# RWKV right sides taken head by head, two chunks in one transposition, and other constants in the order planner

## The chip, the cores and the metric

The kernel runs on one core of one Trainium2 chip. The metric is device time in microseconds (us) of one execution; lower is better. TensorE is called PE here, VectorE DVE, ScalarE ACT, GpSimd POOL and SyncE SP, as in the profile.

## The reference

One inference step of a two-layer encoder, for 528 prompt rows (16 learned meta rows and 512 tokens) and 8 sample streams of 16 rows, all in float32. Each layer computes

```
h = rmsnorm(x); z = h @ w_in                      # one combined projection, 7 input groups
A: RWKV-7 time mixing, 8 heads of 64:
   sa = S @ (-kk);  S = S*decay + sa (kk*a)^T + v k^T;  y = S @ r     # per row
B: latent attention (low-rank K and V, rotary key, QK norm), 8 heads
x += (sigmoid(g_a) * (A @ w_branch_a) + sigmoid(g_b) * (B @ w_branch_b)) @ w_out
```

The prompt starts A from a zero state; each sample stream starts it from its own state (`state_rwkv`, 64x64 for each head), and the final states are outputs. Outputs are also the new caches and the last projected rows.

## The kernel before

All 656 rows (128 sample rows, then the prompt) lie along the free axis, so the activations are tiles of 128 features x 656, cut into halves of 328. The large projections run as three passes in a rounded float format, from a high and a low part of both sides: these are the matmuls on tile `zt` (`main_mm`, line 751), 48 for each 128 output columns of the input projection. Their weights come in as `raw`, ACT and POOL split them into `whi` and `wlo` (`main_split`), and `main_post` (line 789) takes the results out of PSUM. Here this stream is called the main one; everything else is called a side operation.

Branch A runs by pairs of heads, `j` = 0 to 3, beside the main stream. A pair's rows are cut into 11 chunks: chunks 0 and 1 hold 4 sample streams of 16 rows each, chunk 2 the meta rows, chunks 3 to 10 the prompt, 64 rows each. For a pair, `rwkv_prep` makes the scaled keys and decays (tile `ar`) and the chunk matrices `Q`; `rwkv_tok` (line 1476) transposes keys (`kbt`) and values (`vt`, line 1496) into rows by features; `rwkv_inv` inverts the triangular blocks with DVE steps on `LP` and 16- and 32-row matmuls on tile `mg`; `rwkv_chain` (line 1604) walks the prompt chunks (`la`, `so`, `mw`, `ch`); and `rwkv_sample` (line 1724) does chunks 0 and 1:

- The streams' states come in as `sin`, are transposed by four matmuls (PSUM tile `s0`, line 1735; its rows read `s`) and copied by ACT to `S0` (rows read `S`), chunk by chunk.
- The right sides `ra` (line 1741) are a local part, two 64x64 matmuls from `Q` and `SAV` (`local`, line 1592), and a state part, eight matmuls for 4 streams x 2 heads. The state part contracts over 128 rows, both heads' rows at once: the left operand `am` holds zeros in the other head's rows.
- `solve` (line 1582) copies `ra` to `RB` by DVE, multiplies (`sa`), and DVE copies the result into `SAV`. Then come the outputs `yo`, the new states (`sn`, `snew`, `snt`) and their DMAs.

A plain float32 matmul is two passes on PE, so eight matmuls show as 16 instructions; a transposition is one.

What sets the order: while the program is built, class `Clock` plans every engine's order, and that order is then fixed on PE, DVE, ACT and POOL. Each generator is a thread with a rank. At each step the operation that can start first, by the planner's own estimates, is issued; at equal starts a side operation goes ahead of the main stream (rank `MAIN` = 90), then one that needs no other array shape, then the lower rank. One rule turns this round: `lean` (line 388) keeps a sum of the columns PE has done of late. Where a side operation would bring the sum below a floor plus `SPARE`, the planner becomes `tight` and side operations go behind the main stream until the sum is above `AGAIN`. Ranks: pairs `j` (samples `j` + 2.5), the shift rows 4, branch A's norms `RN` = 5, the prompt's attention `RPR` = 5 (`mla_prompt`), the sample's attention 0. The main tasks of a layer come in a fixed order: 23 tasks of the input projection can run during branch A; the gate tasks after them wait for ("rw", l), which is set when all pairs are done (`pre`, line 1045).

PSUM tiles of side operations come from two rings, `s` with 3 banks and `c` with 2 (`PSB`, line 73). `S2` (line 610) takes two banks of ring `s` at once.

Of the kernel before, what the change touches and what calls it, by code (L numbers as in the profile page):

```python
# [10 lines left out]
F32 = mybir.dt.float32  # L11
F32R = mybir.dt.float32r
I32 = mybir.dt.int32
AF = mybir.ActivationFunctionType
ALU = mybir.AluOpType
# [35 lines left out]
DLAT = 1.9  # L51
DRATE = 260e3
MAIN = 90
RPR = 5
RN = 5
RPOST, RSPLIT, RRAW = -3, 0, 2
MARGIN = 0.1
PIN = "PVAG"
TICK = 3.41333
ENTRY = 3100.0  # L60
SPARE = 150.0
AGAIN = 4400.0
GEARLY = 0
GMID = 1
SBB = 1
# [8 lines left out]
CT = "c"  # L74
# [136 lines left out]
class Clock:  # L211
# [176 lines left out]
    def lean(self, o):  # L388
# [8 lines left out]
        if self.tight:  # L397
            self.tight = self.dense(t - TICK) < AGAIN
        elif c < ENTRY + SPARE:
            self.tight = True  # L400
# [171 lines left out]
def trunk_kernel(ctx: ExitStack, tc: tile.TileContext, I, O, dbg=None, nlayers=NL):  # L572
    nc = tc.nc
    clk = Clock(tc)
    V, A, G, TE, SP = (Engine(e, clk, n) for e, n in ((nc.vector, "V"), (nc.scalar, "A"), (nc.gpsimd, "G"), (nc.tensor, "P"), (nc.sync, "S")))
# [17 lines left out]
    def C(name):  # L593
        i, o, n = COFF[name]
        return ctile[i][:, o:o + n]

    ident = C("ident")
# [17 lines left out]

    def S(name="s", tag="s"):
        return pools["PS"].tile([128, 512], F32, tag=tag, name=name, bufs=PSB[tag])
# [17 lines left out]
    def mm(out, lhsT, rhs, start, stop):  # L635
        TE.matmul(out, lhsT, rhs, start=start, stop=stop)
# [729 lines left out]
    def Us(name):  # L1366
        return pools["R"].tile([128, 512], F32, tag="U", name=name, bufs=UR)


    def ccol(c):  # L1370
        return (0, 64, 128)[c] if c < 3 else PR + 64 * (c - 3)
# [104 lines left out]
    def rwkv_tok(l, j):  # L1476
        while ("kb", l, j) not in done:
            yield has(("kb", l, j))
        R = pools["R"]
        kbf, r = st["kbf", j], None  # L1480

        BKT = R.tile([128, 11, 128], F32, tag="BKT", name="BKT", bufs=2)
        st["BKT", j] = BKT
        for cs in ((0, 1, 2, 3), (4, 5, 6, 7), (8, 9, 10)):
            ps = S("kbt")
            for i, c in enumerate(cs):
                TE.transpose(ps[:, 128 * i:128 * i + 128], kbf[:, c, :], ident)
            A.activation(out=BKT[:, cs[0]:cs[-1] + 1, :], in_=ps[:, 0:128 * len(cs)].rearrange("p (a b) -> p a b", b=128), func=AF.Copy)
            yield None
        done.add(("kbt", l, j))  # L1490
        while ("v", l, j) not in done or ("pq", l, j) not in done:
            yield has(("v", l, j), ("pq", l, j))
        v = get(("v", l, j), "K")
        r, SAV = st["r", l, j], st["SAV", j]
        for cs in ((0, 1, 2, 3), (4, 5, 6, 7), (8, 9, 10)):
            ps = S("vt")
            for i, c in enumerate(cs):
                TE.transpose(ps[0:64, 128 * i:128 * i + 128], v[:, ccol(c):ccol(c) + 64], ident)
            A.activation(out=SAV[0:64, cs[0]:cs[-1] + 1].rearrange("p a b c -> p a (b c)"),
                         in_=ps[0:64, 0:128 * len(cs)].rearrange("p (a b) -> p a b", b=128), func=AF.Copy)  # L1500
            yield None

        for hh, (c0, c1) in enumerate(H2):
            ps = S("bo")
            z = [Us("bo")[:, 0:328] for _ in range(2)]
            split(*z, r[:, c0:c1])
            for i in range(2):
                mm(ps[:, 0:328], r_(C("bones")), r_(z[i]), i == 0, i == 1)
            V.tensor_tensor(out=v[:, c0:c1], in0=v[:, c0:c1], in1=ps[:, 0:328], op=ALU.mult)
            yield None  # L1510
        SP.dma_start(out=bod[j], in_=v)
        done.add(("tok", l, j))
# [65 lines left out]
        yield None  # L1578

    PR2 = (slice(0, 64), slice(64, 128))  # L1580

    def solve(j, c, ps):

        Q, SAV = st["Q", j], st["SAV", j]
        rb = pools["R"].tile([128, 128], F32, tag="RB", name="RB", bufs=1)
        V.tensor_copy(out=rb[64:128], in_=ps[64:128, 0:128])
        ps2 = S("sa", CT if c > 1 else "s")
        for p in range(2):
            mm(ps2[64:128, 64 * p:64 * p + 64], Q[64:128, c, p, 0:64], rb[64:128, 64 * p:64 * p + 64], p == 0, p == 1)
        V.tensor_copy(out=SAV[64:128, c].rearrange("p h v -> p (h v)"), in_=ps2[64:128, 0:128])  # L1590

    def local(j, c, ps, stop):
        Q, SAV = st["Q", j], st["SAV", j]
        for p in range(2):
            mm(ps[64:128, 64 * p:64 * p + 64], Q[0:64, c, p, 0:64], SAV[0:64, c, p, :], p == 0, stop and p == 1)

    def chain_y(j, c, ps, n, first):
        Q, SAV = st["Q", j], st["SAV", j]
# [125 lines left out]
    def rwkv_sample(l, j):  # L1724
        R = pools["R"]
        Q, SAV, BKT = st["Q", j], st["SAV", j], st["BKT", j]
        pc = st["pc", j]
        ar = st["ar", j]
        yt = st["y", j]
        for c in range(2):  # L1730
            t = Us("sin")
            for p in range(2):
                SP.dma_start(out=t[0:64].rearrange("v (s h k) -> v s h k", s=4, h=2)[:, :, p],
                             in_=I["state_rwkv"][l, 4 * c:4 * c + 4, 2 * j + p].rearrange("s v k -> v s k"))
            ps = S("s0")
            for s in range(4):
                TE.transpose(ps[:, 64 * s:64 * s + 64], t[0:64, 128 * s:128 * s + 128], ident[0:64, 0:64])
            S0 = R.tile([128, 4, 64], F32, tag="S0", name="S0", bufs=2)
            A.activation(out=S0.rearrange("p s v -> p (s v)"), in_=ps[:, 0:256], func=AF.Copy)
            yield None  # L1740
            ps = S("ra")
            local(j, c, ps, False)
            am = st["am", l]
            for p in range(2):
                V.tensor_copy(out=am[PR2[p], 256 * p:256 * p + 320].rearrange("p (s t) -> p s t", t=80)[:, :, 0:16], in_=ar[PR2[p], 0, 64 * c:64 * c + 64].rearrange("p (s t) -> p s t", t=16))
            for s in range(4):
                for p in range(2):
                    mm(ps[64:128, 64 * p:64 * p + 64], am[:, 256 * p + 64 * s:256 * p + 64 * s + 64], S0[:, s, :], False, p == 1 and s == 3)
            yield None
            solve(j, c, ps)  # L1750
            yield None
            py = S("yo")
            for s in range(4):
                for p in range(2):
                    mm(py[PR2[p], 16 * s:16 * s + 16], S0[PR2[p], s, :], ar[PR2[p], 1, 64 * c + 16 * s:64 * c + 16 * s + 16], s == 0, False)
            chain_y(j, c, py, 64, False)
            A.activation(out=yt[:, 64 * c:64 * c + 64], in_=py[:, 0:64], func=AF.Copy)
            yield None
            sx = Us("sx")
            V.tensor_tensor(out=sx.rearrange("p (h s v) -> p h s v", h=2, v=64),  # L1760
                            in0=SAV[:, c].rearrange("p h (u v) -> p h u v", u=1).to_broadcast([128, 2, 4, 64]),
                            in1=C("rmask").rearrange("p (h s v) -> p h s v", h=1, v=1).to_broadcast([128, 2, 4, 64]), op=ALU.mult)
            psn = S("sn")
            for p in range(2):
                mm(psn[PR2[p], 0:256], BKT[:, c, 64 * p:64 * p + 64], sx[:, 256 * p:256 * p + 256], True, True)
            sn = Us("snew")[:, 0:256]
            o3 = sn.rearrange("p (s v) -> p s v", v=64)
            V.tensor_tensor(out=o3, in0=psn[:, 0:256].rearrange("p (s v) -> p s v", v=64), in1=S0, op=ALU.add)
            G.tensor_tensor(out=o3, in0=o3, in1=pc[:, 4 * c:4 * c + 4].rearrange("p (s u) -> p s u", u=1).to_broadcast([128, 4, 64]), op=ALU.mult)
            yield None  # L1770
            pst = S("snt")
            for s in range(4):
                TE.transpose(pst[0:64, 128 * s:128 * s + 128], sn[:, 64 * s:64 * s + 64], ident)
            so = Us("so")
            A.activation(out=so[0:64], in_=pst[0:64], func=AF.Copy)
            for p in range(2):
                SP.dma_start(out=O[6][l, 4 * c:4 * c + 4, 2 * j + p].rearrange("s v k -> v s k"),
                             in_=so[0:64].rearrange("v (s h k) -> v s h k", s=4, h=2)[:, :, p])
            yield None
        done.add(("samp", l, j))  # L1780
# [694 lines left out]
    def branches(l):  # L2475
# [13 lines left out]
        smp_open(l)  # L2489
        yield from par(mla_sample(l), mla_prompt(l), open_y(l), rank=[0, RPR, 0])  # L2490

# [77 lines left out]
```

## Time and profile before

| | |
|---|---|
| time, median of 3 runs | 1768.52 us (1762.73 to 1777.48) |
| time of the profiled execution | 1768.54 us |
| its span, first to last instruction | 1766.8 us |
| instructions | 38155 |
| mean granted PE clock | 0.954 of full |

In the rows below, the granted clock of 1.00 is 2.4 GHz, and 0.50 is 1.2 GHz. Busy times of PE are modelled ends of pipelined passes, so the start of one group against the start of the next tells what a group costs; the duration shown does not. `128*64` after a matmul is the shape of the array tile that it uses (rows * columns); `(x16)` or `x16` counts instructions. A trailing bracket names idle time before an instruction and what ended it. Branch A of the first layer fills about 88 to 418 us, that of the second about 968 to 1275 us.

### The profile page before, as it was taken

The page shows a single profiled execution, that of the slowest core. Times are in us where ns is not written, and L with a number is a line of the kernel's source. Part 1 is how long each engine was busy: PE and PEld are TensorE (multiplying, and loading weights), DVE is VectorE, ACT ScalarE, POOL GpSimd, SP SyncE. Part 2 cuts the span into 40 slices and gives each one's busy share as a digit, 9 for nine tenths or more (in the row PEclk, how much of TensorE's full clock was granted, in tenths as well). Part 3 has the DMA queues.
Part 4 walks back from the last instruction along what each step waited for, and adds up shares of the span by engine and source line. Part 5 has one row for each costly group of instructions (what it writes and reads, how often), then busy time and mean ns, then how long its engine had stood idle before and what let it go on. Part 6 is the DMA issues. An engine that isn't in the chain of part 4 may idle for free.

```text
span 1766.8 us, 38155 instructions
## 1 busy us (share of the span) xinstructions
PE 1673.0 (95%) x15157; PEld 1507.2 (85%) x15157; DVE 983.8 (56%) x2366; ACT 727.1 (41%) x1704; POOL 578.1 (33%) x590
## 2 busy tenths in 40 slices
PE   7999998999999997999999999899999999899998
PEld 6988777788898996899999878778888999889998
DVE  5686776755552454455336867886456334455441
ACT  4544343443544543223334434455345444432231
POOL 2422122134522533014434212132354244411262
PEclk9998897999999998999999978999999999999999
DMA  6531222235465226365532312232455642356462
GB/s 194 159 112 49 57 77 70 58 108 186 121 215 165 70 72 182 103 176 173 175 107 83 105 35 66 78 91 60 146 180 159 201 124 68 109 164 178 148 211 84
DMA packets 217916, 217.27 MB, mean 123 GB/s; under 512 B 46217, under 2 KB 166481, under 8 KB 217209
## 3 DMA queue, kind: packets, MB, share of 16 engines
q1 hardware_dynamic: 217737, 214.82, 40.4%
q8 instruction: 120, 1.97, 0.5%
q14 instruction: 59, 0.48, 0.1%
HBM read 145.98 MB, written 68.52 MB: 121 GB/s over the span
## 4 chain that ended last, share of the span: by engine, by line
PE 72%; DVE 16%; ACT 4%; issue 3%; DMA 3%; POOL 1%; SPq 1%; DVEq 0%; POOLq 0%; ACTq 0%
PE zt L566 41%; DVE LP L566 3%; PE pv L566 3%; PE st L566 3%; PE mg L566 3%; PE kp L566 3%; PE yo L566 1%; PE pcx L566 1%; PE so L566 1%; PE psc L566 1%; DVE itmp L566 1%; PE pq L566 1%; DVE xs L566 1%; PE ra L566 1%; DMA q<-qpd 1%
## 5 line engine op out<-in xcount | busy, mean ns | idle before, releaser
L566 POOL TENSOR_TENSOR wlo<-raw,whi 128x512 fp32r<-128x512 f32 (+2 forms) x304 | 346.0, 1146 | 669.8 <-ACT whi L566 603.5
L566 PE MATMUL zt<-hhi,whi 128*128 128x328 f32 (+1 forms) x1376 | 453.1, 329 | 6.8 <-ACT whi L566 4.5
L566 PE MATMUL zt<-hhi,wlo 128*128 128x328 f32 (+1 forms) x1376 | 452.7, 329 | 3.6 <-POOL wlo L566 3.6
L566 PE MATMUL zt<-hlo,whi 128*128 128x328 f32 (+1 forms) x1376 | 453.3, 329 | 0.4 <-issue 0.3
L566 PEld LDWEIGHTS zt<-hhi,whi 128*128 128x128 f32 (+1 forms) x1376 | 268.5, 195 | 14.9 <-ACT whi L566 5.4
L566 PEld LDWEIGHTS zt<-hhi,wlo 128*128 128x128 f32 (+1 forms) x1376 | 268.3, 195 | 13.9 <-POOL wlo L566 5.1
L566 PEld LDWEIGHTS zt<-hlo,whi 128*128 128x128 f32 (+1 forms) x1376 | 268.2, 195 | 8.6 <-issue 3.0
L566 ACT ACTIVATE whi<-raw 128x512 fp32r<-128x512 f32 (+2 forms) x304 | 163.7, 551 | 211.6 <-PE zt L566 182.8
L566 DVE TENSOR_TENSOR sg<-zt,rb 128x328 f32<-128x328 f32 x64 | 31.7, 496 | 94.9 <-PE zt L566 94.8
L566 PE MATMUL zt<-mh,wlo 128*128 128x328 f32 x256 | 81.4, 318 | 0.0
L566 PE MATMUL zt<-ml,whi 128*128 128x328 f32 x256 | 80.8, 316 | 0.0
L566 PE MATMUL zt<-mh,whi 128*128 128x328 f32 x256 | 80.2, 313 | 0.0
L566 ACT ACTIVATE xs<-u,vec 128x328 f32<-128x328 f32 x68 | 38.6, 568 | 92.9 <-DVE u L566 90.4
L566 ACT ACTIVATE pT<-st 128x384 f32<-128x384 f32 (+3 forms) x80 | 35.0, 463 | 85.0 <-DVE st L566 48.3
L566 DVE TENSOR_TENSOR kh<-kp,kh 128x272 fp32r<-128x272 f32 x64 | 28.1, 441 | 71.4 <-ACT kh L566 71.2
L566 PE MATMUL st<-q,k 96*128 96x512 f32 (+9 forms) x288 | 65.1, 333 | 1.0 <-DVE st L566 0.6
L566 PE MATMUL zt<-ya,whi 128*128 128x328 f32 x256 | 65.4, 322 | 0.0
L566 DVE SCALAR_TENSOR_TENSOR xs<-u,vec,xs 128x327 f32<-128x327 f32 x68 | 48.2, 709 | 25.4 <-ACT xs L566 19.9
L566 DVE TENSOR_TENSOR xn<-xn,zt 128x328 f32<-128x328 f32 x32 | 15.8, 495 | 77.7 <-PE zt L566 71.4
L566 POOL TENSOR_TENSOR snew<-snew,pc 128x256 f32<-128x256 f32 x16 | 10.8, 672 | 143.1 <-DVE snew L566 143.1
L566 POOL TENSOR_TENSOR sqs<-sqs 128x272 f32<-128x272 f32 x48 | 37.2, 776 | 60.3 <-ACT sqs L566 58.1
L566 PEld LDWEIGHTS pv<-vtok,pT 128*128 128x128 f32 x480 | 55.6, 192 | 0.2
(410 smaller groups left out, 3783.7 us busy)
## 6 DMA issues: line engine op xcount, KB each, us to landing
raw<-in_w_in_dram SPq DMA_DIRECT2D x84, 512.0 KB
raw<-in_w_out_dram SPq DMA_DIRECT2D x16, 512.0 KB
gad<-sg SPq DMA_DIRECT2D x16, 328.0 KB
gbd<-sg SPq DMA_DIRECT2D x16, 328.0 KB
ga<-gad SPq DMA_DIRECT2D x16, 328.0 KB
ya<-yad SPq DMA_DIRECT2D x16, 328.0 KB
mad<-ga SPq DMA_DIRECT2D x16, 328.0 KB
gg<-gbd SPq DMA_DIRECT2D x16, 328.0 KB
```

What stands on the lines that cost most here:

```text
L566: clk.record(n, lambda: f(*a, **kw), outs, ins, c, cols if n == "P" else 0, lock, lane)
```

## The change

Three edits, and constants of the planner:

- `rwkv_tok` transposes the values of two neighbouring chunks at once, 128 columns instead of 64, in 6 instead of 11 transpositions for a pair; ACT takes each chunk from its half of the partitions, in 4 copies instead of 3.
- `rwkv_sample` loads both chunks' states into one tile, chunk 0 in partitions 0 to 63 and chunk 1 in 64 to 127, and transposes both by four matmuls of full height; one ACT copy of 512 columns takes the place of two of 256, and `S0` is one buffer with both chunks.
- The state part of the right sides contracts over 64 rows, each head over its own. Head 0 goes on in the local part's bank (`ps`), head 1 gets a bank of its own (`ps1`). ACT copies `ps` to `RB` and DVE adds `ps1` to head 1's half, where one DVE copy stood.
- `RPR` 5 to 7, `SPARE` 150 to 600, `AGAIN` 4400 to 4800.

```diff
-RPR = 5
+RPR = 7
-SPARE = 150.0
-AGAIN = 4400.0
+SPARE = 600.0
+AGAIN = 4800.0
...
-        for cs in ((0, 1, 2, 3), (4, 5, 6, 7), (8, 9, 10)):
+        for cs in ((3, 5, 7, 9), (0, 2)):
             ps = S("vt")
+            n = len(cs)
             for i, c in enumerate(cs):
-                TE.transpose(ps[0:64, 128 * i:128 * i + 128], v[:, ccol(c):ccol(c) + 64], ident)
-            A.activation(out=SAV[0:64, cs[0]:cs[-1] + 1].rearrange("p a b c -> p a (b c)"),
-                         in_=ps[0:64, 0:128 * len(cs)].rearrange("p (a b) -> p a b", b=128), func=AF.Copy)
+                TE.transpose(ps[:, 128 * i:128 * i + 128], v[:, ccol(c):ccol(c) + 128], ident)
+            p3 = ps[:, 0:128 * n].rearrange("p (a b) -> p a b", b=128)
+            A.activation(out=SAV[0:64, cs[0]:cs[-1] + 1:2].rearrange("p a b c -> p a (b c)"), in_=p3[0:64], func=AF.Copy)
+            m = n if n > 2 else 1
+            A.activation(out=SAV[0:64, cs[0] + 1:cs[0] + 2 * m:2].rearrange("p a b c -> p a (b c)"), in_=p3[64:128, 0:m], func=AF.Copy)
...
-            ps = S("s0")
-            for s in range(4):
-                TE.transpose(ps[:, 64 * s:64 * s + 64], t[0:64, 128 * s:128 * s + 128], ident[0:64, 0:64])
-            S0 = R.tile([128, 4, 64], F32, tag="S0", name="S0", bufs=2)
-            A.activation(out=S0.rearrange("p s v -> p (s v)"), in_=ps[:, 0:256], func=AF.Copy)
-            yield None
-            ps = S("ra")
-            local(j, c, ps, False)
+        ps = S("s0")
+        for s in range(4):
+            TE.transpose(ps[:, 128 * s:128 * s + 128], t[:, 128 * s:128 * s + 128], ident)
+        S0 = R.tile([128, 4, 2, 64], F32, tag="S0", name="S0", bufs=1)
+        A.activation(out=S0.rearrange("p s c v -> p (s c v)"), in_=ps, func=AF.Copy)
+        yield None
+        for c in range(2):
+            ps, ps1 = S2("ra", "ra")
+            for p in range(2):
+                mm(ps[64:128, 64 * p:64 * p + 64], Q[0:64, c, p, 0:64], SAV[0:64, c, p, :], p == 0, False)
...
             for s in range(4):
                 for p in range(2):
-                    mm(ps[64:128, 64 * p:64 * p + 64], am[:, 256 * p + 64 * s:256 * p + 64 * s + 64], S0[:, s, :], False, p == 1 and s == 3)
-            yield None
-            solve(j, c, ps)
+                    mm((ps, ps1)[p][64:128, 0:64], am[PR2[p], 256 * p + 64 * s:256 * p + 64 * s + 64], S0[PR2[p], s, c, :], p == 1 and s == 0, s == 3)
+            yield None
+            rb = R.tile([128, 128], F32, tag="RB", name="RB", bufs=1)
+            A.activation(out=rb[64:128], in_=ps[64:128, 0:128], func=AF.Copy)
+            V.tensor_tensor(out=rb[64:128, 64:128], in0=ps1[64:128, 0:64], in1=rb[64:128, 64:128], op=ALU.add)
+            ps2 = S("sa")
```

The rest of `solve` stands inline as it was, and `solve` and `local` are gone.

## Rows read from the trace of the kernel before

**Rows 1.** the page: engines' busy time, and PE's granted clock in 40 slices
```profile
PE 1673.0 (95%) x15157; PEld 1507.2 (85%) x15157; DVE 983.8 (56%) x2366; ACT 727.1 (41%) x1704; POOL 578.1 (33%) x590
...
PEclk9998897999999998999999978999999999999999
```

**Rows 2.** windows of three stages: us, busy by engine (x instructions), PEclk, DMA
```profile
132.00:352.00 220.00, 202.33 (x2531) 165.84 (x2531) 153.20 (x352) 92.31 (x217) 48.73 (x49) 0.84 0.22 62
...
1012.00:1144.00 132.00, 123.90 (x1617) 101.06 (x1615) 95.26 (x230) 55.05 (x129) 27.77 (x29) 0.86 0.19 55
1144.00:1280.00 136.00, 129.23 (x1648) 106.95 (x1649) 86.87 (x201) 61.81 (x147) 38.68 (x39) 0.99 0.33 99
```

**Rows 3.** the page: chain that ended last, shares of the span by engine
```profile
PE 72%; DVE 16%; ACT 4%; issue 3%; DMA 3%; POOL 1%; SPq 1%; DVEq 0%; POOLq 0%; ACTq 0%
```

**Rows 4.** pieces of the chain of waits, 88 to 400 us: start, us, what
```profile
165.53 0.56 PE vt L566 x4
...
231.96 1.08 PE ra L566 x16
```

**Rows 5.** the same chain, 980 to 1290 us
```profile
1035.23 0.58 PE kbt L566 x4
```

**Rows 6.** timeline, 1258 to 1268 us: start, us, engine, what
```profile
1258.56 0.31 PE L566 MATMUL zt<-hhi,wlo 128*128 128x328 f32 x1
...
1258.70 0.32 PE L566 MATMUL zt<-hhi,whi 128*128 128x328 f32 x1
...
1258.95 0.46 PE L566 MATMUL s<-cst,sin 64*128 64x64 f32 x4
...
1259.34 0.42 PE L566 MATMUL zt<-hlo,whi 128*128 128x328 f32 x1
...
1259.69 0.44 PE L566 MATMUL ra<-QV 64*64 64x64 f32 x4
...
1260.06 0.41 PE L566 MATMUL zt<-hhi,wlo 128*128 128x328 f32 x1
...
1260.40 1.15 PE L566 MATMUL ra<-S,am 128*64 128x64 f32 x16
...
1261.48 0.41 PE L566 MATMUL zt<-hhi,whi 128*128 128x328 f32 x1
...
1261.59 0.29 DVE L566 COPY RB<-ra 64x128 f32<-64x128 f32 x1 [1.67 <-PE ra L566]
```

**Rows 7.** timeline of PE, 384 to 389 us
```profile
384.43 0.27 PE L566 MATMUL so<-LP,QV 64*64 64x128 f32 x1
384.44 0.22 PE L566 MATMUL la<-QV 64*64 64x64 f32 x1
384.54 0.27 PE L566 MATMUL so<-LP,QV 64*64 64x128 f32 x1
```

**Rows 8.** ACT's groups by shape: xcount | busy us, mean ns | idle before
```profile
L566 ACT ACTIVATE LP<-la 64x128 f32<-64x128 f32 x72 | 19.5, 271 | 4.9 <-PE la L566 3.2
...
L566 ACT ACTIVATE QV<-vt 64x512 f32<-64x512 f32 x16 | 9.1, 585 | 1.1 <-PE vt L566 0.9
...
L566 ACT ACTIVATE S<-s 128x256 f32<-128x256 f32 x16 | 6.1, 380 | 6.5 <-PE s L566 6.3
...
L566 ACT ACTIVATE QV<-vt 64x384 f32<-64x384 f32 x8 | 3.9, 481 | 6.1 <-PE vt L566 6.1
```

**Rows 9.** DVE's groups by shape, the one nearest to an addition of 64 columns
```profile
L566 DVE SCALAR_TENSOR_TENSOR SB<-ch,pc,SB 128x64 f32<-128x64 f32 x64 | 17.8, 278 | 5.3 <-PE ch L566 4.4
```

**Rows 10.** windows of 4 us in the first layer's stage
```profile
136.00:140.00 4.00, 2.28 (x73) 2.02 (x71) 3.73 (x7) 1.88 (x6) 1.52 (x2) 1.00 0.46 121
...
144.00:148.00 4.00, 4.00 (x41) 3.59 (x40) 1.98 (x4) 1.31 (x4) 1.97 (x1) 0.50 0.00 0
284.00:288.00 4.00, 1.40 (x11) 1.16 (x11) 3.83 (x5) 1.32 (x3) 0.62 (x1) 1.00 0.51 131
```

**Rows 11.** windows, instructions on zt alone
```profile
88.00:418.00 330.00, 148.27 (x707) 119.09 (x706) 17.75 (x35) 5.22 (x12) 0.90 0.26 76
```

More of the change, by code (lines that the diff above doesn't have):

```diff
@@ L1580, in trunk_kernel @@
     PR2 = (slice(0, 64), slice(64, 128))
[L1582 to L1595, printed above, removed]
     def chain_y(j, c, ps, n, first):
@@ L1729, in rwkv_sample @@
         yt = st["y", j]
+        t = Us("sin")
         for c in range(2):
-            t = Us("sin")
             for p in range(2):
-                SP.dma_start(out=t[0:64].rearrange("v (s h k) -> v s h k", s=4, h=2)[:, :, p],
+                SP.dma_start(out=t[64 * c:64 * c + 64].rearrange("v (s h k) -> v s h k", s=4, h=2)[:, :, p],
                              in_=I["state_rwkv"][l, 4 * c:4 * c + 4, 2 * j + p].rearrange("s v k -> v s k"))
-            ps = S("s0")
-            for s in range(4):
-                TE.transpose(ps[:, 64 * s:64 * s + 64], t[0:64, 128 * s:128 * s + 128], ident[0:64, 0:64])
-            S0 = R.tile([128, 4, 64], F32, tag="S0", name="S0", bufs=2)
-            A.activation(out=S0.rearrange("p s v -> p (s v)"), in_=ps[:, 0:256], func=AF.Copy)
-            yield None
-            ps = S("ra")
-            local(j, c, ps, False)
+        ps = S("s0")
[8 more added lines that the diff above has]
+                mm(ps[64:128, 64 * p:64 * p + 64], Q[0:64, c, p, 0:64], SAV[0:64, c, p, :], p == 0, False)
             am = st["am", l]
@@ L1747, in rwkv_sample @@
                 for p in range(2):
-                    mm(ps[64:128, 64 * p:64 * p + 64], am[:, 256 * p + 64 * s:256 * p + 64 * s + 64], S0[:, s, :], False, p == 1 and s == 3)
+                    mm((ps, ps1)[p][64:128, 0:64], am[PR2[p], 256 * p + 64 * s:256 * p + 64 * s + 64], S0[PR2[p], s, c, :], p == 1 and s == 0, s == 3)
             yield None
-            solve(j, c, ps)
+            rb = R.tile([128, 128], F32, tag="RB", name="RB", bufs=1)
+            A.activation(out=rb[64:128], in_=ps[64:128, 0:128], func=AF.Copy)
+            V.tensor_tensor(out=rb[64:128, 64:128], in0=ps1[64:128, 0:64], in1=rb[64:128, 64:128], op=ALU.add)
+            ps2 = S("sa")
+            for p in range(2):
+                mm(ps2[64:128, 64 * p:64 * p + 64], Q[64:128, c, p, 0:64], rb[64:128, 64 * p:64 * p + 64], p == 0, p == 1)
+            V.tensor_copy(out=SAV[64:128, c].rearrange("p h v -> p (h v)"), in_=ps2[64:128, 0:128])
             yield None
@@ L1754, in rwkv_sample @@
                 for p in range(2):
-                    mm(py[PR2[p], 16 * s:16 * s + 16], S0[PR2[p], s, :], ar[PR2[p], 1, 64 * c + 16 * s:64 * c + 16 * s + 16], s == 0, False)
+                    mm(py[PR2[p], 16 * s:16 * s + 16], S0[PR2[p], s, c, :], ar[PR2[p], 1, 64 * c + 16 * s:64 * c + 16 * s + 16], s == 0, False)
             chain_y(j, c, py, 64, False)
@@ L1767, in rwkv_sample @@
             o3 = sn.rearrange("p (s v) -> p s v", v=64)
-            V.tensor_tensor(out=o3, in0=psn[:, 0:256].rearrange("p (s v) -> p s v", v=64), in1=S0, op=ALU.add)
+            V.tensor_tensor(out=o3, in0=psn[:, 0:256].rearrange("p (s v) -> p s v", v=64), in1=S0[:, :, c, :], op=ALU.add)
             G.tensor_tensor(out=o3, in0=o3, in1=pc[:, 4 * c:4 * c + 4].rearrange("p (s u) -> p s u", u=1).to_broadcast([128, 4, 64]), op=ALU.mult)
```

## The prediction

> **What bounds the kernel now.** I read the page first. PE is busy 95% of the span and no other engine passes 56% [rows 1], so PE's work and PE's clock are the two things to ask about. The row of the granted clock is at 9 or full but for a few slices. The windows by stage place them: in 132 to 352 us the clock is 0.84 and in 1012 to 1144 us 0.86, while 1144 to 1280 us, branch A too, has 0.99 [rows 2]. The two low stretches are in branch A of the two layers, where the three edits lie. The clock has two levels, so a mean of 0.84 over 220 us is 0.16 x 2 x 220 = 70 us at 1.2 GHz, and 0.86 over 132 us is 37 us: 107 us at half rate, worth 54 us of full rate. In the same stretches PE is busy 202.33 of 220 and 123.90 of 132 us, 92% and 94%. So branch A is bound by PE for the most part, with DVE next, and the chain that ended last says the same: PE 72%, DVE 16% [rows 3]. The groups of sixteen `ra` passes stand on that chain: ten of the kernel's 16 are whole pieces of it, eight of them near the 1.08 us of the one that is shown [rows 4], two at half clock longer.
>
> **Right sides.** Two layers, 4 pairs and 2 chunks make 16 groups of 16 state passes. One takes 1.08 us (1260.40 to 1261.48, [rows 6]), 67 ns a pass. Afterwards each pass needs 64 rows, and the heads alternate between the two halves of the array, so two can run together, where both halves write the same output partitions. The trace shows that case: `so` reads the upper rows, `la` the lower ones, both write partitions 64 to 127 of different banks, and `so` starts each 0.11 us with an `la` pass within [rows 7]. An `so` pass moves 128 columns, twice as many as here. If the pair of passes costs those 0.11 us, a group takes 8 x 0.11 = 0.88 us and saves 0.20; if it costs one pass of today, it takes 8 x 0.067 = 0.54 and also saves 0.54. I take 0.54, as 64 columns are what today's passes move too: 16 x 0.54 = 8.6 us. Changes of array shape come on top. From `zt` at 1260.06 to the `ra` group at 1260.40 it is 0.34 us, where a `zt` pass in a row takes 0.14 to 0.15 (1258.56 to 1258.70), so the change costs 0.19 [rows 6]; the local part has a change of its own. With both parts in 64*64 one is saved where they stand together, which the planner decides: between 0 and 16 x 0.19 = 3, I take 1.2. Right sides: 9.8 us, between 3 and 12.
>
> A rule speaks about this edit. The Trainium skill, "TensorEngine Tiling (Array Packing)", Restrictions and Gotchas, says that different row tiles cannot work on one PSUM bank at a time, so that row tiling needs more banks. The pairs in the trace write different tiles, and no run here shows two row halves on one bank. The change gives head 1 its own bank, so by the rule the pairing stands; had both heads shared a bank, the 8.6 us would go and the forecast would be 6 us later.
>
> **States.** A group of four half-height transpositions stands between two `zt` passes: `s` starts at 1258.95, the `zt` behind it at 1259.34 (0.39 us), and 0.10 us of shape change lies before it [rows 6]: 0.49, twice for a pair. Afterwards there are four of full height without a change of shape; four such `kbt` take 0.58 us [rows 5]. That saves 0.98 - 0.58 = 0.40, 8 times: 3.2 us (0 if the trace's 0.49 is mostly drain that stays).
>
> **Values.** Four `vt` take 0.56 us on the chain [rows 4], 0.14 each, and four full ones 0.145 each [rows 5]. A pair had 11 and has 6: 1.54 - 0.87 = 0.67, 8 times: 5.4 us.
>
> **The sum on PE** is 9.8 + 3.2 + 5.4 = 18.4 us, between 8 and 21. Of a saving in a stretch where PE holds 72% of the chain I count 72%: 13.2 us. What is late next, where it doesn't count, is DVE's steps for the inverse, which run with or without these passes.
>
> **ACT and DVE.** For a pair's values ACT keeps two copies of 512 columns, and in place of one of 384 (481 ns) come one of 256 (380, the states' copy is as wide) and one of 128 (271): +0.17 us. For the states 2 x 380 become one of 585: -0.18 us [rows 8]. Together nothing, at an engine that is 41% busy. The right side was taken out by one DVE copy of 295 ns; now an ACT copy of 64x128 (271 ns, [rows 8]) comes first and then a DVE addition of 64x64. The trace has no such addition; the nearest is `SB` with 64 columns from PSUM, 278 ns [rows 9], so I take 0.28, between 0.2 and 0.3. The way to `sa` gets 0.26 us longer, 16 times 4 us. In front of it stand `zt` passes that can run meanwhile (1261.48 and on, behind the copy at 1261.59, [rows 6]); where a stage ends with the last pair's samples that cover thins out, for two chunks in two layers: 4 x 0.26 = 1 us lost. Queued behind the new ACT copy is ACT's weight split for the main stream, later by 0.27 us each time, with two more split buffers ahead of it: nothing, and 16 x 0.27 = 4 us if the main stream were waiting for each.
>
> **DMA and buffers.** The 32 loads of states stay 32; all four of a pair are issued at its start on SP, two earlier than now, ahead of what SP would issue then: nothing. One `S0` buffer in place of two costs nothing, since a pair's samples wait for those of the pair before anyway.
>
> **`RPR` 5 to 7.** Ranks only break ties. While the prompt's heads run, the other threads have rank 0, 2 or below, or 90; the norms with rank 5 end before, because the keys wait for them. No thread lies between 5 and 7, so this does nothing.
>
> **`SPARE` and `AGAIN`.** These put main passes ahead of branch A's sooner and for longer. Where did the clock fall? At 136 to 140 us PE works 2.28 of 4 us, with `mg` passes of 16 and 32 rows behind, and 144 to 148 us is at 0.50; at 284 to 288 us it works 1.40 of 4 [rows 10]. Each fall begins with a gap in which PE had nothing ready, main passes included, while DVE was busy 3.73 and 3.83 us; no order of PE mends that. The half-rate time after it, with main passes and sparse ones mixed, is what a reserve can shorten. Bounds: all 107 us cured gives 54 us; on the other side, 268 us of the second layer (1012 to 1280) at the first layer's 0.84 instead of today's would have 86 us at half rate, where it has 37 + 3, so 23 us lost. That the same program runs at 0.84 in one layer and 0.86 and 0.99 in the other shows how much hangs on the order. I take 5 us gained, near nothing, since the gaps come first.
>
> **Sum.** 13.2 + 5 - 1 = 17 us off the profiled execution's 1768.54 (a span of 1766.8 and 1.7 around it): 1751.5 us. The median of the runs is 1768.52, so it needs no shift.
>
> **Rivals.** First, the saving is eaten. The right sides hold two of the three banks of ring `s` from the local part (1259.69) to the end of the copy (1261.88), 2.2 us [rows 6], and values, keys, `pq` and norms share what is left. If each of the 16 groups makes others wait for 0.8 us, 13 us are gone, and with no help from the clock it ends at 1768. For it: `pq` needs two banks at once. Against it: `vt` and `s0` take 3 uses of a bank for a pair where they took 5, and the main stream has banks of its own. Second, the clock recovers: half of the 107 us is cured, 27 us, with 12 from PE: 1730. For it: half-rate stretches are full of main passes (4.00 us busy in 4, [rows 10]) that could have come earlier. Against it: the gaps. Third, slower: the filler runs out. In 88 to 418 us there are 707 main passes [rows 11], and 23 tasks of 48 make 1104 in all, the rest of which ran before; later tasks wait until branch A is done. A larger reserve spends them sooner. If each layer's last 40 us of branch A are left without filler, PE runs them at half rate: 20 us a layer lost, 40, of which the earlier main passes give back a fourth; with 13 us saved that is 1768.5 + 30 - 13 = 1785.5. It decides once the last main pass of the stage ends before the last pair's inverse. For it: the pool just lasts to the end today. Against it: what goes early raises the clock early.
>
> **How the numbers follow.** Forecast 0.45 (1740 to 1763 is its own range), eaten 0.23, clock recovers 0.17, filler runs out 0.15. A measurement of this kernel tells about 1% from no change, 17.7 us: below 1750.8 is faster, above 1786.2 slower. Faster holds the second rival and a little over half of the forecast: 0.42. Slower is most of the third: 0.12. Between them 0.46. The range goes from a bit under the second rival, 1726, to a bit short of the third's far side, 1782.
>
> **What would show it.** Right: 80 `vt` and `s` transpositions, all at 128*128, instead of 152; `ra` groups of 64*64 with starts 0.5 to 0.6 us apart for 16 passes; PE's busy time in branch A lower by some 18 us; a like granted clock there. Wrong: a granted clock in branch A that moves by more than 0.03, either way, makes the order, not the passes, the main term; `ra` pieces still near 1 us mean that the halves don't run together; PE idle behind `pq` or `ra` means banks.

## The result and the profile after

The changed kernel takes 1718.39 us, median of 4 runs (1714.56 to 1720.23); the kernel before took 1772.66 us beside it (1762.73 to 1777.48, 4 runs). The ratio is 0.9698, 95% interval 0.9647 to 0.9749: 3% faster, 54 us. The forecast of 1751.5 and its range from 1726 to 1782 both lie above it. Ratios here and below are taken from the fast executions alone, so they need not be the quotients of the medians. The profiled execution took 1714.56 us, with a span of 1712.8 and a mean granted clock of 0.965 (before: 1766.8 and 0.954).

The page of the kernel after: busy time of each engine, the granted clock in 40 slices, and the engines' shares of the chain that ended last. They answer to [rows 1] and [rows 3]. This chain can be followed back to 321 us only, so the shares of the last line add to some 80% of the span, where those of [rows 3] add to 100%: they can't be compared one by one.

```profile
PE 1637.0 (96%) x15085; PEld 1480.0 (86%) x15085; DVE 988.8 (58%) x2366; ACT 734.0 (43%) x1720; POOL 578.0 (34%) x590
...
PEclk8998998979999999998999999999999999999999
...
PE 61%; DVE 11%; ACT 2%; issue 2%; DMA 2%; POOL 1%; SPq 1%; DVEq 0%; POOLq 0%; ACTq 0%
```

PE's busy time fell by 36.0 us, though the passes saved account for less than half of that: a pass at half clock counts as busy for nearly twice as long (main passes in a row start 0.15 us apart at full and 0.27 us at half clock, medians in the kernel before). To part the two, I split each span in three: PE's idle time (span less busy time), the time lost at half rate ((1 - mean clock) x span), and the rest, the work at full rate.

| us | span | PE idle | lost at half rate | work |
|---|---|---|---|---|
| before | 1766.8 | 93.8 | 81.3 | 1591.7 |
| after | 1712.8 | 75.8 | 59.9 | 1577.1 |
| difference | -54.0 | -18.0 | -21.4 | -14.6 |

The mean clock has three digits, which leaves 0.9 us either way in the last two columns. Idle time at half rate stands in both of the first two terms, 2 to 10 us in the kernels below, so that the work comes out too low by as much; counted once, the work of these two kernels differs by 17.8 us.

Windows of the kernel after, the three of [rows 2] (start:end in us, then length, busy us of PE, PEld, DVE, ACT, POOL with instructions, granted clock, DMA share, GB/s):

```profile
132.00:352.00 220.00, 207.36 (x2844) 170.94 (x2843) 164.24 (x378) 107.53 (x250) 57.19 (x59) 0.91 0.25 74
1012.00:1144.00 132.00, 122.08 (x1575) 101.03 (x1574) 105.82 (x249) 64.66 (x150) 36.29 (x37) 0.92 0.26 79
1144.00:1280.00 136.00, 132.74 (x1648) 109.10 (x1648) 86.96 (x199) 65.19 (x177) 50.15 (x65) 1.00 0.42 130
```

The granted clock of the first went from 0.84 to 0.91 and that of the second from 0.86 to 0.92. But branch A is not where most of the time came from. Two instructions mark the stages: the load `c<-seld` ends branch A, and the first `zt<-mh` ends a layer's attention. Before, they stood at 425.3, 847.1, 1281.3 and 1761.0 us (the last `zt<-mh` for the second layer); after, at 405.7, 815.7, 1248.5 and 1706.9. So the four stages changed by -19.6, -11.8, -1.4 and -21.3 us: 33 of the 54 us came from the two attention stages, where none of the three edits lies (the planner's constants act there too).

There, one place stands out. When the sample's attention ends and the prompt's heads begin (the first `sc` pass), PE needs main passes to fill the waits. Windows of the kernel before around it, first all instructions (the 40 us around the first `sc` pass of either layer at the end), then those on `zt` alone (without a column for POOL):

```profile
660.00:684.00 24.00, 23.80 (x174) 23.10 (x173) 7.93 (x20) 10.31 (x24) 10.64 (x10) 1.00 0.31 100
690.00:708.00 18.00, 9.89 (x44) 7.99 (x42) 9.39 (x40) 2.65 (x8) 3.76 (x10) 0.53 0.94 253
...
676.20:716.20 40.00, 26.43 (x143) 22.03 (x142) 20.10 (x74) 10.80 (x29) 8.87 (x16) 0.77 0.70 205
...
1526.70:1566.70 40.00, 34.84 (x230) 32.67 (x229) 22.00 (x73) 14.47 (x36) 15.13 (x21) 0.91 0.63 191
...
660.00:684.00 24.00, 18.89 (x111) 16.87 (x111) 4.01 (x8) 1.77 (x4) 1.00 0.31 100
684.00:724.00 40.00, 1.12 (x5) 0.77 (x5) 0.99 (x2) 0.44 (x1) 0.70 0.61 175
```

Up to 684 us there are 111 main passes in 24 us; then 5 in 40. PE works 9.89 of the 18 us from 690 to 708, at 0.53 of full clock, and the chain shows what it waits for: short steps of `kp`, ACT, DVE and `psc`, then one DMA. The chain of the kernel before, 684 to 702 us (start, us, what):

```profile
686.79 0.77 PE kp L566 x6
687.58 0.41 ACT kh L566
688.00 0.45 DVE kh L566
688.50 0.53 PE psc L566 x2
689.16 0.58 SPq L566
689.78 6.25 DMA q<-qpd
696.17 0.46 PE sc L566
```

In the kernel after, the same handover lies at 661 and 1492 us. Its windows, all instructions and those on `zt`:

```profile
640.00:680.00 40.00, 37.78 (x259) 34.88 (x257) 21.86 (x69) 15.22 (x38) 14.56 (x19) 1.00 0.64 195
1472.00:1512.00 40.00, 37.01 (x261) 34.49 (x260) 23.74 (x75) 16.90 (x41) 17.45 (x22) 1.00 0.64 192
...
640.00:680.00 40.00, 25.13 (x143) 21.93 (x143) 6.47 (x13) 2.94 (x7) 1.00 0.64 195
1472.00:1512.00 40.00, 24.22 (x128) 19.76 (x128) 5.94 (x12) 2.66 (x6) 1.00 0.64 192
```

143 and 128 main passes, full clock, 2 to 3 us idle. The main passes run out because the tasks behind the last `gb` task wait until the samples' attention is done. In the first layer both kernels have the same stock for this stage, 1099 and 1100 main passes from the end of branch A to the first `ya` pass; up to 20 us ahead of the first `sc` pass the kernel before has spent 1064 of them, the kernel after 959. Idle time and half-rate loss in the 40 us around the first `sc` pass are 22.8 and 8.8 us in the two layers before, 2.2 and 3.0 after: 26 of the 39 us by which these two terms fell in all.

### The profile page after: what moved, and what is told of

It reads as the page before. It is cut to its first block, busy times and chain, and to the rows that moved or that the text cites. A ratio compares the mean times of both kernels' runs of the same rounds, so it can differ in the third digit from the quotient of the medians.

```text
span 1712.8 us, 38032 instructions
## 1 busy us (share of the span) xinstructions
PE 1637.0 (96%) x15085; PEld 1480.0 (86%) x15085; DVE 988.8 (58%) x2366; ACT 734.0 (43%) x1720; POOL 578.0 (34%) x590
## 4 chain that ended last, share of the span: by engine, by line
PE 61%; DVE 11%; ACT 2%; issue 2%; DMA 2%; POOL 1%; SPq 1%; DVEq 0%; POOLq 0%; ACTq 0%
PE zt L566 37%; PE kp L566 3%; PE st L566 3%; PE pv L566 2%; DVE LP L566 2%; PE mg L566 2%; PE psc L566 1%; DVE rs_u L566 1%; PE pcx L566 1%; DMA q<-qpd 1%; PE yo L566 1%; DVE itmp L566 1%; SPq L566 1%; PE vps L566 1%; PE so L566 1%
## 5 line engine op out<-in xcount | busy, mean ns | idle before, releaser
L566 PE MATMUL zt<-hhi,whi 128*128 128x328 f32 (+1 forms) x1376 | 447.1, 325 | 4.0 <-ACT whi L566 1.7
L566 PE MATMUL zt<-mh,wlo 128*128 128x328 f32 x256 | 81.4, 318 | 0.0
L566 PE MATMUL zt<-ml,whi 128*128 128x328 f32 x256 | 80.8, 316 | 0.0
L566 DVE TENSOR_TENSOR xn<-xn,zt 128x328 f32<-128x328 f32 x32 | 15.9, 496 | 77.2 <-PE zt L566 70.9
L566 PE MATMUL pv<-vtok,pT 128*128 128x65 f32 x480 | 57.7, 279 | 0.0
```

The lines of the kernel that those rows point to most:

```text
L566: clk.record(n, lambda: f(*a, **kw), outs, ins, c, cols if n == "P" else 0, lock, lane)
```

## The experiments

All kernels compute the whole result. The table gives their medians, the ratio to the kernel before on the same chip, and the split of the profiled span, which is one execution out of those behind the median. "Old constants" are `RPR` 5, `SPARE` 150, `AGAIN` 4400. `RPR` alone leaves the program as it was, instruction for instruction, in either kernel; it has no run of its own. `DLAT` (1.9) and `MARGIN` (0.1) are the planner's estimates of a DMA's latency and of a wait before a side pass on PE; changing them changes no instruction, only the order.

| run | us (range, runs) | ratio [95%] | idle | half rate | work |
|---|---|---|---|---|---|
| const_only | 1767.33 (1753.45-1769.34, and one execution of 3768.61; 7) | 0.9964 [0.9924, 1.0003] | 81.4 | 98.9 | 1585.1 |
| ra_only | 1754.38 (1751.26-1756.98, 4) | 0.9880 [0.9854, 0.9906] | 85.7 | 85.9 | 1582.0 |
| trans_only | 1737.78 (1728.43-1747.07, 4) | 0.9789 [0.9746, 0.9833] | 84.7 | 67.6 | 1581.9 |
| struct_only | 1725.23 (1716.99-1728.36, 4) | 0.9712 [0.9681, 0.9743] | 73.0 | 77.5 | 1572.2 |
| before_twice | 1785.52 (1776.44-1801.10, 10) | 1.0059 [1.0018, 1.0101] | 86.9 | 98.2 | 1600.7 |
| after_twice | 1709.59 (1703.21-1713.15, 4) | 0.9619 [0.9563, 0.9675] | 64.0 | 56.4 | 1588.7 |
| before_dma2 | 1778.32 (1775.12-1787.18, 10) | 1.0030 [1.0000, 1.0061] | 80.8 | 115.6 | 1582.0 |
| before_margin | 1740.54 (1738.25-1742.41, 4) | 0.9846 [0.9791, 0.9902] | 73.7 | 69.5 | 1594.0 |
| before_dma18 | 1757.54 (1744.34-1766.31, 10) | 0.9919 [0.9881, 0.9956] | 81.8 | 87.7 | 1585.2 |
| struct_dma2 | 1756.44 (1741.07-1760.37, 4) | 0.9885 [0.9822, 0.9948] | 85.2 | 109.0 | 1564.4 |
| struct_margin | 1726.74 (1723.92-1730.39, 4) | 0.9731 [0.9675, 0.9786] | 75.3 | 82.9 | 1569.0 |
| struct_dma18 | 1743.78 (1729.97-1761.77, 4) | 0.9804 [0.9737, 0.9870] | 88.0 | 70.9 | 1569.3 |
| after_dma2 | 1773.53 (1765.87-1787.04, 10) | 1.0033 [0.9995, 1.0070] | 97.1 | 99.3 | 1576.5 |
| after_margin | 1751.14 (1743.91-1762.33, 9) | 0.9891 [0.9850, 0.9932] | 92.1 | 84.0 | 1574.2 |
| after_dma18 | 1728.55 (1723.72-1731.42, 4) | 0.9784 [0.9716, 0.9853] | 79.0 | 65.4 | 1577.5 |
| after_spare450 | 1747.96 (1742.77-1756.85, 4) | 0.9858 [0.9805, 0.9912] | 92.6 | 93.0 | 1569.5 |
| dma2_hold2 | 1767.57 (1756.58-1779.57, 10) | 0.9988 [0.9949, 1.0028] | 95.6 | 97.2 | 1574.9 |
| dma2_hold4 | 1766.68 (1753.34-1774.30, and one execution of 2680.14; 10) | 0.9960 [0.9926, 0.9995] | 95.7 | 90.0 | 1578.5 |

**The change in its parts.** `const_only` is the kernel before with the three new constants, `struct_only` the three edits with the old ones, `ra_only` the right sides alone and `trans_only` the transpositions of values and states alone, both with the old constants.

```diff
 const_only
-RPR = 5
+RPR = 7
...
-SPARE = 150.0
+SPARE = 600.0
-AGAIN = 4400.0
+AGAIN = 4800.0
 struct_only, against the kernel after
-RPR = 7
+RPR = 5
...
-SPARE = 600.0
+SPARE = 150.0
-AGAIN = 4800.0
+AGAIN = 4400.0
```

> The kernel before with SPARE 600, AGAIN 4800 and RPR 7 alone. Theory 'order' (the constants gave the clock and the idle time, the passes only their own 15 us): about 39 us faster than before, near 1733, with a granted clock of branch A above 0.90. Rival 'passes' (the fewer passes gave nearly all): within 8 us of before, 1765 to 1780. Rival 'draw' (every new plan falls at random by some 15 us): anywhere from 1745 to 1790, without relation to the sum of the parts.

> The three edits of the right sides, states and values with the constants of before. 'Order': 13 to 18 us faster than before, 1755 to 1760. 'Passes': about 50 us faster, near 1722. 'Draw': anywhere from 1735 to 1775, and with const_only the two don't add to 54.

> Only the right sides head by head, on the kernel before. By my sum on PE 9.8 us x 0.72 = 7 us faster, near 1765; the groups of 16 passes 0.55 to 0.65 us apart from the next. 'Passes' wants 25 us or more. 'Draw' leaves 1745 to 1785 open.

> Only states and values of two chunks in one transposition, on the kernel before. By my sum on PE 8.6 us x 0.72 = 6 us faster, near 1766. 'Passes' wants 20 us or more. 'Draw' leaves 1745 to 1785 open.

The work of the two halves falls by 9.7 and 9.8 us, and that of all three edits by 19.5, against the kernel before (9.7, 14.4 and 23.3 with idle time at half rate counted once): about the size that was expected of the passes. The times do not follow the work. Against the median of 1773.01 us that the kernel before had beside them, `ra_only` is 19 us faster for 9.7 us of work, `trans_only` 35 for 9.8, and all three edits 48 for 19.5. What differs is idle time and half rate, which moved by -3.5, -22.8 and -24.6 us. The constants alone are within 1%. Taken by themselves these four runs fit the rival 'passes' best: const_only stays within 8 us of before, struct_only lies near 1722, and the two add to 54 us, which 'draw' had denied; only the 19 us of ra_only miss the 25 that 'passes' wanted. But each of them is one order out of many.

**The passes, doubled.** To price the transpositions with the order held fixed, `after_twice` issues each of its 80 `vt` and `s` transpositions twice, the second copy right behind the first into the same place; `before_twice` does so with its 152. The planner does not see the copies, so that the order of everything else is the same.

```diff
-        ins = o.call()
+        for ins in (o.call() for _ in range(o.nm)):
...
+                clk.twice = 2
                 TE.transpose(ps[:, 128 * i:128 * i + 128], v[:, ccol(c):ccol(c) + 128], ident)
```

> The changed kernel with each of its 80 value and state transpositions issued twice in a row. The planner doesn't know of the second ones, so the order of every engine stays as it is and only PE's work grows, by 80 x 0.11 to 0.145 = 9 to 12 us. Theory 'amplified' (a pass taken out of branch A gives two or three times its own time, since idle and half-rate time go with it): 20 to 35 us slower than the changed kernel, 1738 to 1753. Rival 'plan' (the passes give their own time and no more, the rest of the 54 us came with another order): 7 to 13 us slower, 1725 to 1731.

> The kernel before with each of its 152 value and state transpositions issued twice, order unchanged: 152 x 0.10 to 0.13 = 15 to 20 us of PE. 'Amplified': 35 us slower or more, above 1805. 'Plan': 11 to 22 us slower, 1784 to 1795.

Groups of the tiles `vt` and `s` in `after_twice` (instructions, then least, median and greatest duration in ns, first and last start in us, form):

```profile
L566 PE MATMUL vt<-cst,ld x72: 272/273/329, 163.3 to 1162.4; 128*128 128x128 f32 x72
...
L566 PE MATMUL vt<-cst,xs x24: 270/272/273, 96.0 to 931.9; 128*128 128x128 f32 x24
...
L566 PE MATMUL s<-cst,sin x64: 270/273/329, 160.3 to 1203.5; 128*128 128x128 f32 x64
```

The 160 transpositions are there, and the work rose by 11.6 us, 0.145 for each copy, the price that the prediction took from [rows 5]. The kernel did not get slower, though both theories wanted that: its median is 9 us lower, with intervals of the two ratios that overlap, and idle time and half rate fell by 15.3 us. The 152 copies in the kernel before cost 9.0 us of work and 12 us of time, as 'plan' expected and far from the 35 of 'amplified'; 0.06 for a copy is less than the 0.14 of [rows 4], by an amount that the work term's own scatter (below) covers. So these runs do not contradict the price of the passes, though they can't fix it closer than that scatter, and one order of instructions, with a little useless work put in, can lose less to idle time and half rate, by as much as that work costs or more.

**The same work in other plans.** If the time lies in the plan, plans that differ by chance should differ by as much as the two kernels do. Three settings put the planner's estimates a little off, each in the kernel before, the changed kernel and the three edits with the old constants; one more run changes `SPARE`. The instructions of every engine stay the same, only their order changes.

```diff
 *_dma2
-DLAT = 1.9
+DLAT = 2.0
 *_dma18
-DLAT = 1.9
+DLAT = 1.8
 *_margin
-MARGIN = 0.1
+MARGIN = 0.12
 after_spare450
-SPARE = 600.0
+SPARE = 450.0
```

> The kernel before, its work unchanged, with another plan: the planner's estimate of a DMA's latency (DLAT) 2.0 in place of 1.9. It measures how far a new plan moves the time by itself. 'Amplified' wants it within 8 us of before, 1765 to 1781. 'Plan' says that plans differ by tens of us: outside of that, either way.

> The changed kernel with the same other plan (DLAT 2.0). 'Amplified': within 8 us of the changed kernel, 1710 to 1726. 'Plan': that kernel had a lucky plan, so this one is slower by more than 8 us.

> The kernel before, same work, another plan (MARGIN 0.12 in place of 0.10). Two theories now. 'Shift': the change moves plans as a body by 30 us or more, and the one slow plan of the changed work (1773) was an exception: then this lies at 1765 to 1785, and after_margin at 1710 to 1735. 'Spread': plans of the same work lie over some 60 us, the change moves their middle only by its own work, about 15 us, and its plan was a good one out of many: then this can lie anywhere from 1735 to 1795.

> The changed kernel, same work, MARGIN 0.12. 'Shift': 1710 to 1735. 'Spread': anywhere from 1715 to 1780, its difference from 1718 shown as PE's idle time and half-rate time, with the rest (span less both) within 10 us of the changed kernel's 1578.

> The kernel before, same work, DLAT 1.8. 'Shift': 1765 to 1785. 'Spread': 1735 to 1795.

> The changed kernel, same work, DLAT 1.8. 'Shift': 1710 to 1735. 'Spread': 1715 to 1780, with idle and half-rate time carrying the difference.

> The three edits with SPARE 150 and AGAIN 4400, DLAT 2.0. If the reserve works, this is slower than after_dma2 (1773) by 10 us or more. If the constants are one draw among others, the four pairs of old against new constants (1725 to 1718 is the first) have no common sign and lie 1710 to 1780; with 1773 at the high end already, this one is more likely below it.

> The three edits with the old constants, MARGIN 0.12. Reserve works: above 1760 (after_margin: 1751). One draw among others: 1710 to 1780.

> The three edits with the old constants, DLAT 1.8. Reserve works: above 1738 (after_dma18: 1728.5). One draw among others: 1710 to 1780.

> The changed kernel with a reserve of 450 in place of 600. A reserve with a smooth effect puts it within 8 us of 1718; one draw among others: 1710 to 1780. In both the span less idle and half-rate time is 1570 to 1580.

These were the runs that decided. With 0.1 us more in one estimate the changed kernel goes from 1718 to 1774 us, the time of the kernel before. Over plans of the old work (before, const_only and its three variants) the work is 1582 to 1594 us, mean 1587.6; over the nine plans of the changed work 1564 to 1578, mean 1572.2. The two groups do not overlap, and their means differ by 15.4 us; with the same estimates on both sides the difference is 5.5 to 25 us. Idle time and half rate together are 143 to 196 us (mean 173) with the old work and 136 to 196 (mean 167) with the changed: they scatter over 50 to 60 us in both, and the 6 us between the means are far inside that. The kernel after, with 135.7, is the lowest of its nine; the kernel before, with 175.1, stands in the middle of its five. Each split is that of one execution, and executions of one order differ too, by 16 to 25 us from the fastest to the slowest of before on one chip; the medians in the table scatter as the splits do. Their means over the same plans, 1763 and 1741 us, are 22 us apart with a standard error of 9: over plans the change is worth about what was forecast, and the 54 us are this pair of plans.

The constants show no gain of their own: against `struct` with the same estimates, `after` is 7 us faster, 17 slower (`dma2`), 24 slower (`margin`) and 15 faster (`dma18`); by the ratios to the kernel before beside each, the two gains shrink to 2 and 4 us, within the intervals. A working reserve wanted struct_dma2, struct_margin and struct_dma18 above 1783, 1760 and 1738 us; only the third is. A reserve of 450 with a smooth effect wanted 1710 to 1726 and gave 1748. The edits have a sign: `struct` against `before` gives -48, -22, -14 and -14 us by the medians, -51, -26, -20 and -20 by the ratios.

Not every run fell as the theory of plans expected: before_dma2 is within 8 us of before, as 'amplified' had it, and after_dma18 fits 'shift' as well as 'spread'. after_dma2, before_margin, after_margin and before_dma18 lie where only plans that scatter put them.

**Where the main passes lie.** Over the 18 kernels run up to here (16 plans, as the doubled ones keep theirs), two layers each, the 40 us around the first `sc` pass of a layer lose 1 to 9 us to idle time and half rate where 120 or more main passes lie in them, 14 to 16 us where there are 72 to 95, and 19 to 33 us where there are 0 to 40. The loss at both handovers, 4 to 47 us, goes with idle time and half rate of the whole span over the 16 plans (correlation 0.84); what is left of these two terms elsewhere is 123 to 167 us, without such a trend. That is a correlation; the last two runs put it to the test. They take the slow plan after_dma2, whose second handover has no main pass and loses 31.2 us, and hold back its last 2 or 4 `gb` tasks (96 or 192 passes) until the samples' attention is done. The order up to the hold is the same.

```diff
 dma2_hold4, against after_dma2 (hold2: j == 2)
-            win_task(l, CGB + 128 * j, gbpost, sets=[("gb", l, j)])
+            win_task(l, CGB + 128 * j, gbpost, sets=[("gb", l, j)], pre=[has(("smp", l, 5))] if l == 1 and j == 0 else [])
```

> The changed kernel with DLAT 2.0, the same order as in after_dma2 up to the hold; then the last 2 gb tasks of the second layer (96 zt passes) wait until the last sample group of attention is done, so that they run at the handover to the prompt's heads. Theory A (where the filler lies decides): in the 40 us around the second layer's first sc pass, after_dma2 has no zt pass and loses 31 us to idle PE and half rate; with the hold it loses under 15, and the time falls by 10 to 20 us, to 1753 to 1763. Rival B (the filler is short in all, the hole only moves): idle and half rate turn up before the release instead, in the attention of the samples, and the time stays within 5 us of 1773.5 or gets longer.

> As dma2_hold2, with all 4 gb tasks of the second layer (192 zt passes) held. Theory A: at least as much as with two, 10 to 25 us less than after_dma2, 1748 to 1763, with over 100 zt passes in the 40 us around the first sc pass and under 8 us lost there. Rival B: the hole before the release grows by what is won behind it, within 5 us of 1773.5 or longer.

Windows of after_dma2, all instructions and then those on `zt`; the first `sc` pass stands at 1549 us:

```profile
1440.00:1480.00 40.00, 39.87 (x297) 38.39 (x297) 15.65 (x41) 20.65 (x51) 18.89 (x19) 1.00 0.30 82
1480.00:1520.00 40.00, 37.66 (x284) 35.51 (x283) 25.39 (x74) 19.97 (x53) 15.61 (x15) 1.00 0.29 88
1520.00:1560.00 40.00, 27.66 (x136) 22.01 (x135) 12.38 (x46) 11.33 (x29) 14.78 (x22) 0.67 0.46 142
...
1480.00:1520.00 40.00, 20.70 (x107) 16.13 (x106) 4.27 (x9) 1.78 (x4) 1.00 0.29 88
1520.00:1560.00 40.00, 2.12 (x12) 1.81 (x12) 1.00 (x2) 0.44 (x1) 0.67 0.46 142
```

The same windows of dma2_hold4, `sc` at 1541 us:

```profile
1440.00:1480.00 40.00, 35.27 (x250) 30.64 (x250) 15.59 (x43) 20.55 (x53) 18.11 (x18) 1.00 0.24 61
1480.00:1520.00 40.00, 29.59 (x206) 25.65 (x205) 20.93 (x64) 16.45 (x47) 12.65 (x14) 0.91 0.09 25
1520.00:1560.00 40.00, 38.71 (x273) 36.82 (x273) 21.63 (x71) 15.06 (x37) 13.83 (x18) 1.00 0.66 198
...
1480.00:1520.00 40.00, 2.00 (x12) 1.78 (x13) 0.00 (x0) 0.00 (x0) 0.91 0.09 25
1520.00:1560.00 40.00, 28.77 (x162) 24.64 (x161) 6.47 (x13) 2.94 (x7) 1.00 0.66 198
```

The handover is mended: 157 main passes around it, and 1.3 us lost in place of 31.2 (with two tasks held, 82 passes and 12.0 us). But a hole opens before the release: from 1440 to 1520 us PE is idle for 15.1 us in place of 2.5 and loses 3.6 at half rate in place of none, 16 us in all. By the medians the time falls by 6 and 7 us, by the ratios to the kernel before by 8 and 13, with intervals of 7 us either way. Theory A's marks at the handover were met (under 15 and under 8 us lost, over 100 passes with four tasks held), its times were not (1767.57 and 1766.68 us for at most 1763). Rival B's hole ahead of the release came, but it wanted a gain of 5 us at the most. It came out between them: by these windows 30 us of loss went at the handover and 16 came ahead of the release. Main passes at the handover are worth their place, and this plan also has too few of them left for its whole attention stage.

Where they went is seen by counting `zt` passes in the 160 us after branch A of the second layer, before any hold acts:

```profile
1277.00:1317.00 40.00, 34.75 (x194) 31.15 (x194) 1.00 (x2) 10.38 (x28) 0.91 0.65 214
1317.00:1357.00 40.00, 32.33 (x197) 29.63 (x197) 4.16 (x9) 0.00 (x0) 1.00 0.47 142
1357.00:1397.00 40.00, 38.27 (x241) 36.19 (x240) 5.22 (x11) 0.00 (x0) 1.00 0.67 211
1397.00:1437.00 40.00, 32.83 (x201) 30.63 (x202) 3.98 (x8) 0.00 (x0) 1.00 0.62 175
```

That is after_dma2, 833 passes. The kernel after, the same 160 us of its own stage:

```profile
1248.00:1288.00 40.00, 34.54 (x218) 31.67 (x219) 1.58 (x4) 10.24 (x28) 1.00 0.67 216
1288.00:1328.00 40.00, 31.06 (x183) 27.47 (x183) 3.46 (x7) 0.00 (x0) 1.00 0.54 166
1328.00:1368.00 40.00, 31.91 (x194) 29.28 (x194) 3.96 (x8) 0.00 (x0) 1.00 0.59 185
1368.00:1408.00 40.00, 26.67 (x158) 23.51 (x157) 3.50 (x7) 0.00 (x0) 1.00 0.49 128
```

753 passes. Up to the first `ya` pass the stage has 1097 here and 1075 in after_dma2, so that some 100 more are left for later, and the first `sc` pass comes 244 us after the stage opens, not 272. All instructions together keep PE busy for 158.6 of these 160 us in the slow plan and for 156.1 here: against 80 more main passes stand 2.4 us more of busy PE there, and the passes are missing at the handover. Which of the planner's choices starts this stays open; it would take a kernel that paces the main passes over the whole stage.

## Why the prediction was wrong, point by point

- **PE passes: right, as closely as the scatter lets it be read.** The predicted 18.4 us, between 8 and 21, stand against 19.5 (struct_only) and 14.6 (after) of work, 15.4 as the mean over plans. By parts, right sides 9.7 measured for 9.8, and values with states 9.8 for 8.6; as plans of one work differ by 12 and 13 us in this term, so close a match of the parts is luck. The pairing of the two halves shows as expected. Timeline of PE in the kernel after, 166.8 to 167.8 us:

```profile
166.82 0.68 PE L566 MATMUL ra<-S,am 64*64 64x64 f32 x16
167.43 0.42 PE L566 MATMUL zt<-hlo,whi 128*128 128x328 f32 x1
167.78 1.08 PE L566 MATMUL so<-LP,QV 64*64 64x128 f32 x8
```

  Sixteen passes and the change of shape behind them take 0.61 us from start to start, where [rows 6] had 1.08: 0.47 saved, 16 times 7.5 us for the 8.6 that were predicted. The passes of the kernel before start 58 to 59 ns apart; these start 7 and 52 ns apart by turns, two in the time of one, while the change of shape behind them keeps its 0.15 us. The prediction had halved that too. The Trainium skill's rule on row tiles and banks ("TensorEngine Tiling (Array Packing)", Restrictions and Gotchas) agrees so far as the trace goes: with a bank for each head the two halves run together; no run put both on one bank. The groups of `ra` that are pieces of the chain are 0.60 to 0.70 us long, and 0.91 in one at half clock. (On the chain of the kernel before, eleven of the 16 groups are whole pieces, where the prediction counted ten.)
- **ACT and DVE: right, by the sizes.** Groups of tiles `RB` and `s` in the kernel after:

```profile
L566 ACT ACTIVATE RB<-ra x16: 260/273/273, 168.4 to 1222.6; 64x128 f32<-64x128 f32 x16
L566 DVE TENSOR_TENSOR RB<-ra,RB x16: 227/227/229, 168.7 to 1223.3; 64x64 f32<-64x64 f32 x16
...
L566 ACT ACTIVATE S<-s x8: 591/597/601, 165.1 to 1208.8; 128x512 f32<-128x512 f32 x8
```

  The addition took 0.227 us for the 0.28 assumed; the way to `sa` grew by 0.273 + 0.227 - 0.295 = 0.2 us. Whether the 1 us that was booked for it was paid can't be told beside a scatter of 60.
- **`RPR`: right.** It changes no engine's order.
- **Banks (first rival): not seen.** PE's idle time just before `pq` and `ra` passes is 3.7 us in the kernel before and 3.9 in the kernel after, where the rival wanted 13 more.
- **Filler (third rival): the mechanism is real, the place was wrong.** In branch A main passes did not run out: 86 and 104 of them lie in the last 40 us of the two stages in the kernel after. They run out at the handover inside attention, and it is the kernel before that had this loss, 31.6 us of it. "The filler runs out" was priced only as something that the change could bring.
- **The step that failed** is the one under `SPARE` and `AGAIN`: "no order of PE mends that", with 5 us gained, "near nothing, since the gaps come first". It took PE's idle time as given and the half-rate time as nearly so. They moved by 18.0 and 21.4 us. Two things were wrong in it. It read windows of branch A only, while the attention stages hold 33 of the 54 us and the single largest loss of the kernel before. And it laid the clock at the door of the constants, which show no gain of their own over four pairs, while edits that leave every engine's instructions as they are, of 0.02 or 0.1 us in an estimate, drew a new plan too, and the plans lie up to 60 us apart in idle time and half rate. Of the 39 us, about 6 is what the means over plans differ by, and the rest is the luck of this draw against that one.
- **The factor of 72%** stays open: 13.2 and 18.4 us are nearer to each other than the time of two plans of one work, so no run here tells them apart.
- **The warning held.** The prediction said that a granted clock in branch A that moves by more than 0.03 makes the order the main term; it moved by 0.07 and 0.06. What it lacked was a range for that term. One from rows was at hand: idle time and half rate together were 175 us of the span, and both could have been given bounds from stage to stage.

The fastest kernel measured is `after_twice`, 1709.59 us. It is the changed kernel in its own order with useless work in it, so it shows that the order still loses time that need not be lost, rather than a change to keep.

## What to carry to other kernels

Where an order is planned on the host, an edit changes two things, the work and the draw of the plan; split the span into idle time, half-rate loss and work before crediting the edit, and time the same edit under several harmless changes of the planner's estimates. Read the clock and PE's idle time over the whole span, not only in the stage that is edited: the filler that is spent early can be missing later, as at the handover here. A kept part of the gain here is the 15 us of work; the other 39 hang on a plan that 0.1 us of an estimate undoes.

## What had not been expected of the hardware

- Twice the transpositions, 80 more passes and 11.6 us more work, left the kernel no slower at the same order (its median is 9 us lower): PE's idle time fell from 75.8 to 64.0 us.
- With both row halves in use and a bank for each, 64x64 passes start 0.61 / 16 = 38 ns apart, change of shape included, where the 128-row passes with zeros in half of their rows needed 67 ns. Without the change the starts are 7 and 52 ns apart by turns, against 58 to 59.
- Executions of one and the same order differ by the clock they are granted: of ten of dma2_hold2 the fastest had a span of 1754.8 us at a mean clock of 0.954, the slowest 1777.8 at 0.937.
